# Keys, queries and output gates of an mLSTM: from wide products to seven block products of half the width

## The chip, the cores and the metric

One core of a Trainium2 chip runs the whole program. The metric is the device time of one execution in microseconds (us); the time before is the median of three runs. Engines: TensorE (PE, matmuls), VectorE (DVE), ScalarE (ACT), GpSimd (POOL), and SyncE (SP), which here only issues DMAs.

## The reference, cut to what matters

The program is two blocks of layers over 512 tokens of width 1024. The change concerns one layer of the second block, the mLSTM mixer:

```python
p = h @ w_in                       # 512 x 1024 times 1024 x 3088
q, k, v, o, ig, fg = jnp.split(p, [hk, 2*hk, 2*hk + D, 2*hk + 2*D, 2*hk + 2*D + 8], axis=-1)   # hk = 512, D = 1024
ig = 15 * tanh((ig + b) / 15);  logf = log_sigmoid(15 * tanh((fg + b) / 15))      # 8 heads
...
decay = exp(bcum_i - bcum_j + ii_j - m)          # causal, per head
scores = (q @ k.T) * decay
hh = rmsnorm((scores @ v + ...) / max(|den|, exp(-m)))
out = (sigmoid(o) * hh * hnorm_g) @ w_out
```

The values v (1024 columns), the keys and queries (512 each), the output gates o (1024) and the sixteen gate columns are all products of the same 512 x 1024 input h.

## The kernel before

All matmuls keep float32 accuracy by three passes: each operand is split (`split`, lines 189 to 192) into a rounded high part (ACT cast, L191) and the rest (DVE subtraction, L192), and `mm3` (lines 286 to 289) issues hi x hi (L287), hi x lo (L288) and lo x hi (L289). The transposed input lies in SBUF as `xt_hi` and `xt_lo`, 128 x 8 x 512, all eight pieces of the width times all tokens. Weights come by DMA in pieces of 512 KB into slots of a pool named `mid` (27 slots of 128 x 1024 floats, shared between lists "a" and "w"; `mid.share` moves slots between the lists).

A framework's scheduler lists the instructions of each engine once, before the run; on the chip each engine takes its list strictly in that order, waiting on semaphores. An instruction that waits therefore holds all behind it on its engine. The order around the change comes from the order of calls in `mlstm` and from the scheduler's own estimates.

In `mlstm` the calls run: `values()` (eight products, L1203 to L1206); `gates()`, whose `proj16` multiplies x by the 16 gate columns (16 matmuls, L242 to L245, then an add on DVE, L248) and whose chain runs on DVE and ACT (L1218 to L1241: tanh, log-sigmoid, a cumulative sum and a running maximum over 512 tokens by two scans, transposes); `keys(0)` and `out_gates(0)`; `attend(0)`; `keys(1)`, `out_gates(1)`; `attend(1)`. The scheduler lays some of the second half's products into attend(0).

`keys` and `out_gates` call `dense`: for each pair of 128-column tiles eight pieces of the width, three passes, each matmul 128 x 128 by 512 tokens. A call of either makes four such tiles: 4 x 8 x 3 = 96 matmuls of 512 columns; the four calls make 384.

Elsewhere (in the two `ffn` layers) the kernel has a second way to make products, `seven` (lines 380 to 445): it cuts x (by tokens and width) and the weight (by width and columns) into 2 x 2 blocks and forms seven block products instead of eight. A product is 2 x 4 x 3 = 24 matmuls of 256 columns, seven make 168. The weight's combinations are made on POOL (L411, L415, L420, L425, each a subtraction of two 128 x 1024 tiles in SBUF) and split like any weight; the results are summed out of PSUM on DVE (L421 to L441). The combinations of x are made once for all products by `Sums` (lines 352 to 375): two subtractions or additions on POOL (L363, L367), eight on DVE (L364 to L375, with four splits), the last of them written over `xt_hi` and `xt_lo` themselves.

The mlstm layer also carries a side job: `ada_sum(l, part)` accumulates a vector times a weight matrix on DVE (L573, 16 steps of 128 x 512, with a 256 KB DMA each), in steps that `ada_go` draws off at set places.

Of the kernel before, what the change touches and what calls it, by code (L numbers as in the profile page):

```python
# [13 lines left out]
AF = mybir.ActivationFunctionType  # L14
# [3 lines left out]
SEQ = 512  # L18
# [12 lines left out]
def kernel(ctx: ExitStack, tc: tile.TileContext, inp: dict, out: bass.AP):  # L31
# [88 lines left out]
    def blk(i):  # L120
        return slice(i * P, (i + 1) * P)
# [7 lines left out]
    def by_block(ap):  # L129
        return ap.rearrange("p (c t) -> p c t", t=P)  # L130
# [210 lines left out]
    def out_half(nk, o, ws):  # L341

        b = out_bank.next()
        for k in range(nk):
            mm3(b, *o(k), *ws(k), k == 0, k == nk - 1)
        return b
# [199 lines left out]
    def ada_open():  # L546
        ada_acc.extend(small.new("m", [512]) for _ in range(2))
        ada_in.append(Ring([small.new("m", [512]) for _ in range(2)]))
# [354 lines left out]
    def ple(l, then):  # L903
        small.share(c=11, f=6)
        mid.share(w=25, a=2)
        pT = [mid.new("a", [2, SEQ], F32R) for _ in range(2)]
        for tb in range(NB):
            t = small.new("f", [256])
            nc.sync.dma_start(t, inp["p"][l, 0, blk(tb), :])
            b = aux_bank.next()  # L910
            for c in range(2):
                T.transpose(b[:, blk(c)], t[:, blk(c)], ident)
            split(pT[0][:, :, blk(tb)], pT[1][:, :, blk(tb)], by_block(b[:, 0:256]))
            small.free(t)
        wp = [Weight(inp["ple_w"][l], 0, 2, [(hf * 512, 512)]) for hf in range(2)]
        ws = [Weight(inp["ple_gate_w"][l], 0, KD, [(hf * 512, 512)]) for hf in range(2)]
        for tb in range(NB):
            need(tb)
            sq = tiny(2)
            for hf in range(2):  # L920
                pw = out_half(2, lambda k: (pT[0][:, k, blk(tb)], pT[1][:, k, blk(tb)]), wp[hf])
                b = proj_tokens(ws[hf], tb, 512)
                sg = small.new("c", [512])

                S.activation(sg, b, AF.Tanh, scale=0.5)
                V.scalar_tensor_tensor(sg, sg, 1.0, pw, op0=add, op1=mult)
                xb = X[:, tb, half(hf)]
                V.scalar_tensor_tensor(xb, sg, 0.5, xb, op0=mult, op1=add)
                small.free(sg)
                then.half(tb, hf, sq)  # L930
            then.block(tb, sq)
        for w in (*wp, *ws):
            w.free()
        mid.free(*pT)
# [257 lines left out]
    def mlstm(then):  # L1192
# [5 lines left out]
        def values():  # L1198
            vs = [[small.new("f", [4, 129]) for _ in range(NB)] for _ in range(2)]
            for v in (*vs[0], *vs[1]):  # L1200
                G.memset(v[:, :, 128:129], 1.0)
            ws = [Weight(w_in, 0, KD, [(1024 + 512 * hg, 512)]) for hg in range(2)]
            for tb in range(NB):  # L1203
                need(tb)
                for hg in range(2):
                    S.copy(vs[hg][tb][:, :, 0:128], by_block(proj_tokens(ws[hg], tb, 512)))  # L1206
            for w in ws:
                w.free()
            return vs

        MX = mid.new("a", [2, SEQ], F32R)

        def gates():
            nc.sync.dma_start(b_if[0:16, :], inp["a_b_if_2"].rearrange("o n -> n o"))
            g16, t1, lf, bcum, cc, mx, one_row = rows = [small.new("c", [SEQ]) for _ in range(7)]
            fg = one_row
            a = proj16(w_in, 3072)
            V.tensor_scalar(g16[0:16, :], a[0:16, :], b_if[0:16, :], 1.0 / 15, op0=add, op1=mult)  # L1218
            S.activation(g16[0:16, :], g16[0:16, :], AF.Tanh)
            V.tensor_scalar(g16[0:16, :], g16[0:16, :], 15.0, None, op0=mult)  # L1220
# [22 lines left out]
            small.free(*rows)  # L1243

        def keys(hg):
            QT, KT = mid.new("a", [2, SEQ]), mid.new("a", [2, SEQ])
            for c0, dst, sc in ((256 * hg, QT, 1.0), (512 + 256 * hg, KT, 0.125)):
                bs = dense(w_in, 0, KD, [(c0, 256)], by_feat, (0, 1), 4)
                for c in range(2):
                    S.activation(dst[:, c, :], bs[c], AF.Copy, scale=sc)  # L1250
            return QT, KT

        def out_gates(hg):
            SG = Quad()
            for c in range(4):
                if c % 2 == 0:
                    bs = dense(w_in, 0, KD, [(2048 + 512 * hg + 128 * c, 256)], by_feat, (0, 1), 4)
                S.activation(SG[c], bs[c % 2], AF.Tanh, scale=0.5)
                V.tensor_scalar(SG[c], SG[c], 1.0, hn_half[:, 4 * hg + c : 4 * hg + c + 1], op0=add, op1=mult)
            return SG  # L1260

        def attend(hg, QT, KT, vv, SG, O):
# [49 lines left out]
            small.free(*vv)  # L1312
            SG.free()

        vv0, vv1 = values()
        mid.share(w=9, a=18)
        gates()
        ada_open()
        ada_sum(0, 4)
        qk0 = keys(0)  # L1320
        SG0 = out_gates(0)
        O = [Parts(), None]
        ada_cols(0, 4)
        ada_sum(0, 2)
        attend(0, *qk0, vv0, SG0, O[0])
        qk1 = keys(1)
        SG1 = out_gates(1)
        O[1] = Parts()
        attend(1, *qk1, vv1, SG1, O[1])
        mid.free(MX)  # L1330
        mid.share(w=19, a=8)
# [248 lines left out]
    rope_tables()  # L1580
    ple(0, NextX())
    dsa()
    ple(1, NextH(0, 0))
    mlstm(NextH(0, 2))
    ffn(0, NextH(1, 0))
    sgu(NextH(1, 2))
# [34 lines left out]
```

## Time and profile before

| | us |
|---|---|
| median of three runs (2270.41, 2270.75, 2275.05) | 2270.75 |
| the profiled execution | 2271.98 |
| its span in the trace | 2270.3 |
| mean granted clock of TensorE, share of full | 0.993 |
| PE busy | 2225.2 (98%) |
| DVE busy | 1466.6 (65%) |
| ACT busy | 974.1 (43%) |
| POOL busy | 237.1 (10%) |

The span is the time from the program's first to its last instruction in the trace; the run's own time is 1.7 us more. Busy shares are means over all layers, so what a change in one layer is worth must be read from that layer's stretch of the timeline: the mlstm's from the end of its values (1042.4) to the end of attend(1) (1203.2).

### The profile page before, as it was taken

The page shows a single profiled execution, that of the slowest core. Times are in us where ns is not written, and L with a number is a line of the kernel's source. Part 1 is how long each engine was busy: PE and PEld are TensorE (multiplying, and loading weights), DVE is VectorE, ACT ScalarE, POOL GpSimd, SP SyncE. Part 2 cuts the span into 40 slices and gives each one's busy share as a digit, 9 for nine tenths or more (in the row PEclk, how much of TensorE's full clock was granted, in tenths as well). Part 3 has the DMA queues.
Part 4 walks back from the last instruction along what each step waited for, and adds up shares of the span by engine and source line. Part 5 has one row for each costly group of instructions (what it writes and reads, how often), then busy time and mean ns, then how long its engine had stood idle before and what let it go on. Part 6 is the DMA issues. An engine that isn't in the chain of part 4 may idle for free.

```text
span 2270.3 us, 29339 instructions
## 1 busy us (share of the span) xinstructions
PE 2225.2 (98%) x11112; PEld 1825.5 (80%) x11112; DVE 1466.6 (65%) x2610; ACT 974.1 (43%) x1784; POOL 237.1 (10%) x209
## 2 busy tenths in 40 slices
PE   8999999999999999999999999999998999999998
PEld 6787788787777777887777888988787888898996
DVE  5655655844895857852637847767657748664765
ACT  4333344424344644343445534435524335443543
POOL 0000000100000000000211121312102201031130
PEclk9999999999999999999999999999999999999999
DMA  5343424322221124223413444352344534322322
GB/s 168 117 121 111 146 82 125 102 70 66 74 84 66 47 80 145 91 76 107 144 51 123 157 129 139 121 163 99 102 146 152 177 124 140 111 85 93 118 94 77
DMA packets 158063, 251.16 MB, mean 111 GB/s; under 512 B 13785, under 2 KB 59057, under 8 KB 157921
## 3 DMA queue, kind: packets, MB, share of 16 engines
q1 hardware_dynamic: 157920, 249.29, 34.7%
q8 instruction: 87, 1.43, 0.3%
q14 instruction: 56, 0.45, 0.1%
HBM read 247.15 MB, written 2.10 MB: 110 GB/s over the span
## 4 chain that ended last, share of the span: by engine, by line
PE 75%; DVE 11%; DMA 6%; ACT 3%; issue 3%; POOL 1%; SPq 0%; DVEq 0%; POOLq 0%; ACTq 0%
PE bank L287 22%; PE bank L288 22%; PE bank L289 22%; DMA small<-in_ada_w_dram 4%; DVE mid L192 4%; DVE small L573 2%; PE bank L1109 2%; PE bank L294 1%; ACT mid L191 1%; PE bank L1288 1%; POOL tiny_c L480 1%; PE bank L1293 1%; PE bank L1124 1%; DMA mid<-in_ffn_w_dram 1%; DMA mid<-in_b_w_in_dram 1%
## 5 line engine op out<-in xcount | busy, mean ns | idle before, releaser
L192 DVE TENSOR_TENSOR mid<-mid,mid 128x512 fp32r<-128x512 f32 (+2 forms) x530 | 514.2, 990 | 460.8 <-ACT mid L191 290.7
L191 ACT CAST mid<-mid 128x512 fp32r<-128x512 f32 (+2 forms) x530 | 420.0, 818 | 755.4 <-DMA mid<-in_ffn_w_dram 142.8
L287 PE MATMUL bank<-mid,mid 128*128 128x512 f32 (+1 forms) x1320 | 492.3, 373 | 6.5 <-DVE small L441 2.7
L288 PE MATMUL bank<-mid,mid 128*128 128x512 f32 (+1 forms) x1320 | 488.9, 370 | 1.5 <-DVE mid L192 1.5
L289 PE MATMUL bank<-mid,mid 128*128 128x512 f32 (+1 forms) x1320 | 488.1, 370 | 0.0
L287 PE MATMUL bank<-xt_hi,mid 128*128 128x512 f32 (+1 forms) x1216 | 428.6, 353 | 4.6 <-DVE small L1435 2.3
L289 PE MATMUL bank<-xt_hi,mid 128*128 128x512 f32 (+1 forms) x1216 | 426.1, 350 | 1.8 <-DVE mid L192 1.8
L288 PE MATMUL bank<-xt_lo,mid 128*128 128x512 f32 (+1 forms) x1216 | 425.6, 350 | 0.0
L287 PEld LDWEIGHTS bank<-mid,mid 128*128 128x128 f32 x1320 | 248.3, 188 | 55.7 <-DVE small L441 3.6
L288 PEld LDWEIGHTS bank<-mid,mid 128*128 128x128 f32 x1320 | 248.1, 188 | 45.6 <-DVE mid L192 2.1
L289 PEld LDWEIGHTS bank<-mid,mid 128*128 128x128 f32 x1320 | 248.1, 188 | 45.4
L287 PEld LDWEIGHTS bank<-xt_hi,mid 128*128 128x128 f32 x1216 | 230.1, 190 | 40.4 <-issue 5.1
L289 PEld LDWEIGHTS bank<-xt_hi,mid 128*128 128x128 f32 x1216 | 230.4, 190 | 34.4 <-DVE mid L192 2.4
L288 PEld LDWEIGHTS bank<-xt_lo,mid 128*128 128x128 f32 x1216 | 230.7, 190 | 32.2 <-issue 1.3
L287 PE MATMUL bank<-mid,xt_hi 128*128 128x512 f32 (+1 forms) x640 | 252.6, 395 | 0.0
L288 PE MATMUL bank<-mid,xt_hi 128*128 128x512 f32 (+1 forms) x640 | 250.4, 391 | 0.1
L289 PE MATMUL bank<-mid,xt_lo 128*128 128x512 f32 (+1 forms) x640 | 250.2, 391 | 0.0
L573 DVE SCALAR_TENSOR_TENSOR small<-small,c_act,small 128x512 f32<-128x512 f32 x168 | 134.1, 811 | 70.5 <-DMA small<-in_ada_w_dram 69.4
L289 PEld LDWEIGHTS bank<-mid,xt_lo 128*128 128x128 f32 x640 | 120.6, 188 | 26.7
L288 PEld LDWEIGHTS bank<-mid,xt_hi 128*128 128x128 f32 x640 | 120.7, 189 | 25.9 <-DVE mid L192 0.5
L287 PEld LDWEIGHTS bank<-mid,xt_hi 128*128 128x128 f32 x640 | 120.8, 189 | 25.3
L480 POOL TENSOR_TENSOR tiny_c<-tiny_c,minus_half 128x1 f32<-128x1 f32 (+1 forms) x68 | 54.5, 804 | 723.9 <-DVE tiny_c L494 377.2
(299 smaller groups left out, 2307.1 us busy)
## 6 DMA issues: line engine op xcount, KB each, us to landing
mid<-in_ffn_w_dram SPq DMA_DIRECT2D x128, 512.0 KB, 3.8
small<-in_ada_w_dram SPq DMA_DIRECT2D x192, 256.0 KB, 2.9
mid<-in_dsa_w_in_dram SPq DMA_DIRECT2D x36, 512.0 KB, 3.5
mid<-in_gla_w_in_dram SPq DMA_DIRECT2D x32, 512.0 KB, 4.3
mid<-in_b_w_in_dram SPq DMA_DIRECT2D x32, 512.0 KB, 3.7
mid<-in_a_w_in_dram SPq DMA_DIRECT2D x24, 512.0 KB, 3.8
mid<-in_gla_w_in_dram SPq DMA_DIRECT2D x32, 256.0 KB, 3.0
mid<-in_gla_w_out_dram SPq DMA_DIRECT2D x16, 512.0 KB, 3.7
```

The lines of the kernel that those rows point to most:

```text
L191: S.copy(hi, src)
L192: V.tensor_sub(lo, src, hi.bitcast(F32))
L287: T.matmul(o, lhsT=lh, rhs=rh, start=start, stop=False)
L288: T.matmul(o, lhsT=lh, rhs=rl, start=False, stop=False)
L289: turns.passed(o, T.matmul(o, lhsT=ll, rhs=rh, start=False, stop=stop))
L294: i = T.transpose(b[:, blk(c)], src, ident)
L480: G.tensor_tensor(r, v, minus_half[:, 0:m], op=ALU.pow)
L573: V.scalar_tensor_tensor(a, t, ck, a, op0=mult, op1=add)
L1109: T.matmul(b[:, :n], lhsT=QT[tb][:, blk(c)], rhs=KT[:, :n], start=True, stop=True)
L1124: T.transpose(b[:, blk(c)], es[c][:, blk(j)], ident)
L1288: T.matmul(sb[:, :n], lhsT=KT[pr, c // 2, blk(j)], rhs=QT[pr, c // 2, j * P :], start=True, stop=True)
L1293: T.matmul(nb[i // 2][:, (i % 2) * 129 : (i % 2) * 129 + 129], lhsT=Dm[j][:, blk(i - j)], rhs=vv[j][:, c, :], start=j == 0, stop=j == i)
```

## The change

`keys` and `out_gates` call `seven` in place of `dense`: four calls, 28 block products. `Sums()` is built behind the values and `proj16` and ahead of the chain of the gates (`gates(a16)`), and is freed behind the fourth call; both `attend` calls come after all of it. The side job's parts (0, 4) and (0, 2) are drawn off earlier, three steps at a time, in `ple(1)` and in `values`. The numbers of slots are other ones.

```diff
         def keys(hg):
-            QT, KT = mid.new("a", [2, SEQ]), mid.new("a", [2, SEQ])
-            for c0, dst, sc in ((256 * hg, QT, 1.0), (512 + 256 * hg, KT, 0.125)):
-                bs = dense(w_in, 0, KD, [(c0, 256)], by_feat, (0, 1), 4)
-                for c in range(2):
-                    S.activation(dst[:, c, :], bs[c], AF.Copy, scale=sc)
-            return QT, KT
+            QK = mid.new("a", [2, SEQ]), mid.new("a", [2, SEQ])
+
+            def done(t, n, b):
+                S.activation(QK[n][:, :, 256 * t : 256 * t + 256], b.rearrange("p (c t) -> p c t", c=2), AF.Copy, scale=(1.0, 0.125)[n])
+                small.free(b)
+
+            seven(w_in, 256 * hg, 512 + 256 * hg, sums, done)
+            return QK
 
         def out_gates(hg):
             SG = Quad()
-            for c in range(4):
-                if c % 2 == 0:
-                    bs = dense(w_in, 0, KD, [(2048 + 512 * hg + 128 * c, 256)], by_feat, (0, 1), 4)
-                S.activation(SG[c], bs[c % 2], AF.Tanh, scale=0.5)
-                V.tensor_scalar(SG[c], SG[c], 1.0, hn_half[:, 4 * hg + c : 4 * hg + c + 1], op0=add, op1=mult)
+
+            def done(t, n, b):
+                S.activation(SG.ts[n][:, :, 256 * t : 256 * t + 256], b.rearrange("p (c t) -> p c t", c=2), AF.Tanh, scale=0.5)
+                small.free(b)
+                if t != n:
+                    for c in (2 * n, 2 * n + 1):
+                        V.tensor_scalar(SG[c], SG[c], 1.0, hn_half[:, 4 * hg + c : 4 * hg + c + 1], op0=add, op1=mult)
+
+            seven(w_in, 2048 + 512 * hg, 2304 + 512 * hg, sums, done)
             return SG
...
+        ada_sum(0, 2, lambda: None)
+        ada_rate[0] = 3
         vv0, vv1 = values()
-        mid.share(w=9, a=18)
-        gates()
-        ada_open()
-        ada_sum(0, 4)
+        a16 = proj16(w_in, 3072)
+        ada_go()
+        ada_rate[0] = 0
+        mid.share(w=12, a=15)
+        sums = Sums()
         qk0 = keys(0)
+        gates(a16)
         SG0 = out_gates(0)
-        O = [Parts(), None]
-        ada_cols(0, 4)
-        ada_sum(0, 2)
-        attend(0, *qk0, vv0, SG0, O[0])
         qk1 = keys(1)
         SG1 = out_gates(1)
-        O[1] = Parts()
+        sums.free()
+        mid.share(w=10, a=17)
+        O = [Parts(), Parts()]
+        attend(0, *qk0, vv0, SG0, O[0])
         attend(1, *qk1, vv1, SG1, O[1])
```

What the layer now calls (unchanged, line numbers of before):

```python
# Sums.__init__ (lines 362 to 376); G is POOL, V is DVE, split is ACT then DVE
G.tensor_tensor(s2, lf[1][0], lf[1][1], op=add)        # L363
V.tensor_add(s1, hf[1][0], hf[1][1])                   # L364
V.tensor_add(s1, s1, s2)
split(*s[0], s1)
G.tensor_tensor(s3, lf[0][0], lf[1][0], op=sub)        # L367
V.tensor_sub(s2, s1, hf[0][0])                         # L368
V.tensor_sub(s2, s2, lf[0][0])
split(*s[1], s2)
V.tensor_sub(s1, hf[0][0], hf[1][0])                   # L371
V.tensor_add(s3, s3, s1)
split(*s[2], s3)
V.tensor_sub(s1, hf[0][1], s2)                         # L374
V.tensor_add(s1, s1, lf[0][1])
split(h[1][0], l[1][0], s1)

# seven, its first half
b11, b12, b22, b21 = load(0, c0), load(0, c1), load(1, c1), load(1, c0)
p = parts(b11)
G.tensor_tensor(b12, b12, b11, op=sub)                 # L411
...
S.copy(m1, product("11", p))
t2 = mid.new("w", [4, 256])
G.tensor_tensor(t2, b22, b12, op=sub)                  # L415
p = parts(b12)
...
p5 = product("s1", p)
p = parts(t2)
G.tensor_tensor(b11, t2, b11, op=sub)                  # L420
V.tensor_add(u, product("s2", p), m1)
...
```

How the lists of the engines changed. First DVE, from the gate columns' add backward (L248; its input comes from `proj16`). Before, three weight splits stand ahead of it:

```order
L192 TENSOR_TENSOR mid_561_8271<-mid_559_8269,mid_560_8270 128x1024
L192 TENSOR_TENSOR mid_564_8301<-mid_562_8299,mid_563_8300 128x1024
L192 TENSOR_TENSOR mid_567_8333<-mid_565_8331,mid_566_8332 128x1024
L248 TENSOR_TENSOR small_355_8202<-small_355_8202,bank0_61 16x512
L1218 TENSOR_SCALAR small_347_8175<-small_355_8202,b_if_157 16x512
```

In the change, the same place (mid_558, 560 and 562 are the low parts of the sums s1, s2, s3; mid_573 is the low part of b11, mid_576 that of b12 - b11):

```order
L364 TENSOR_TENSOR mid_563_8283<-xt_hi_70 128x1024
L365 TENSOR_TENSOR mid_563_8283<-mid_563_8283,mid_564_8284 128x1024
L368 TENSOR_TENSOR mid_564_8284<-mid_563_8283,xt_hi_70 128x1024
L192 TENSOR_TENSOR mid_558_8278<-mid_563_8283,mid_557_8277 128x1024
L369 TENSOR_TENSOR mid_564_8284<-mid_564_8284,xt_lo_71 128x1024
L371 TENSOR_TENSOR mid_563_8283<-xt_hi_70 128x1024
L192 TENSOR_TENSOR mid_573_8315<-mid_568_8306,mid_572_8314 128x1024
L192 TENSOR_TENSOR mid_560_8280<-mid_564_8284,mid_559_8279 128x1024
L372 TENSOR_TENSOR mid_565_8285<-mid_565_8285,mid_563_8283 128x1024
L192 TENSOR_TENSOR mid_576_8349<-mid_569_8308,mid_575_8348 128x1024
L248 TENSOR_TENSOR small_352_8274<-small_352_8274,bank0_61 16x512
```

Where three DVE operations on 128 x 1024 tiles stood ahead of the gates' add, there are ten in the change; the one that PE's first block product reads (mid_576) is the tenth.

PE behind `proj16` (its last two matmuls are L244 and L245). Before, the first product of the keys:

```order
L245 MATMUL bank0_61<-xt_hi_70,n16_72 48x512
L287 MATMUL bank1_62<-xt_hi_70,mid_560_8270 128x512
L288 MATMUL bank1_62<-xt_lo_71,mid_560_8270 128x512
L289 MATMUL bank1_62<-xt_hi_70,mid_561_8271 128x512
```

In the change (mid_557 and mid_558 are s1's two parts, mid_575 and mid_576 those of b12 - b11):

```order
L245 MATMUL bank0_61<-xt_hi_70,n16_72 48x512
L287 MATMUL bank1_62<-mid_557_8277,mid_575_8348 128x256
L288 MATMUL bank1_62<-mid_558_8278,mid_575_8348 128x256
L289 MATMUL bank1_62<-mid_557_8277,mid_576_8349 128x256
L287 MATMUL bank1_62<-mid_557_8277,mid_575_8348 128x256
...
L287 MATMUL bank0_61<-xt_hi_70,mid_572_8314 128x256
L288 MATMUL bank0_61<-xt_lo_71,mid_572_8314 128x256
L289 MATMUL bank0_61<-xt_hi_70,mid_573_8315 128x256
```

The product with s1 stands ahead of the one with x's own block (mid_572, mid_573), although `seven` is written the other way round; its third matmul reads mid_576.

ACT ahead of the first exponential of `attend(0)` (L1285 before, L1292 in the change). Before:

```order
L191 CAST mid_598_8836<-mid_597_8835 128x1024
L1258 ACTIVATE mid_572_8394<-bank1_62 128x512
L1285 ACTIVATE small_360_8573<-bank4_65,c_cols_158 128x512
```

In the change (mid_658, mid_661 and mid_664 are raw pieces of `w_out`, loaded into slots that the sevens give back; mid_665 is the cast of the third):

```order
L1260 ACTIVATE mid_629_9023<-small_372_9038 128x2x256
L191 CAST mid_659_9677<-mid_658_9676 128x1024
L1260 ACTIVATE mid_630_9024<-small_375_9187 128x2x256
L191 CAST mid_662_9695<-mid_661_9694 128x1024
L1260 ACTIVATE mid_629_9023<-small_373_9039 128x2x256
L191 CAST mid_665_9713<-mid_664_9712 128x1024
L1260 ACTIVATE mid_630_9024<-small_374_9125 128x2x256
L1292 ACTIVATE small_376_9264<-bank4_65,c_cols_158 128x512
```

Before, one cast of a weight of the same products stands there; in the change three casts of `w_out`'s pieces, the third of which waits for a DMA that can start only when a late product has given its slot back.

## Rows read from the trace of the kernel before

**Rows 1.** The profile's page, its parts 1 and 4 (busy time; share of the chain).

```profile
PE 2225.2 (98%) x11112; PEld 1825.5 (80%) x11112; DVE 1466.6 (65%) x2610; ACT 974.1 (43%) x1784; POOL 237.1 (10%) x209
...
PE 75%; DVE 11%; DMA 6%; ACT 3%; issue 3%; POOL 1%; SPq 0%; DVEq 0%; POOLq 0%; ACTq 0%
```

**Rows 2.** Windows: length, busy (x) of PE, PEld, DVE, ACT, POOL, clock, DMA share, GB/s.

```profile
1046.20:1094.50 48.30, 47.96 (x211) 37.14 (x209) 18.57 (x23) 18.89 (x25) 0.52 (x1) 1.00 0.36 105
1094.50:1133.40 38.90, 37.56 (x185) 25.76 (x184) 29.55 (x62) 17.75 (x64) 11.72 (x20) 1.00 0.52 160
1133.40:1167.20 33.80, 33.80 (x148) 27.14 (x146) 10.18 (x12) 11.13 (x15) 0.00 (x0) 1.00 0.22 74
1167.20:1203.20 36.00, 35.54 (x158) 24.01 (x158) 20.20 (x44) 18.47 (x64) 9.55 (x20) 0.91 0.13 44
1344.10:1384.30 40.20, 39.97 (x338) 39.71 (x336) 31.65 (x31) 25.12 (x35) 10.67 (x4) 1.00 0.32 105
2005.90:2045.90 40.00, 39.85 (x337) 39.60 (x336) 31.50 (x31) 25.06 (x35) 10.57 (x4) 1.00 0.33 105
```

**Rows 3.** Timeline of PE, end of the values, the gates' projection, first keys: start, us.

```profile
1035.44 0.40 PE L287 MATMUL bank<-mid,xt_hi 128*128 128x512 f32 x1
...
1042.40 0.40 PE L245 MATMUL bank<-xt_hi,n 128*48 128x512 f32 x1
...
1046.11 0.39 PE L287 MATMUL bank<-xt_hi,mid 128*128 128x512 f32 x1
```

**Rows 4.** Timeline of POOL in ffn(0): start, us, line, operation.

```profile
1280.98 2.42 POOL L367 TENSOR_TENSOR mid<-xt_lo 128x1024 f32<-128x1024 f32 x1 [12.96 <-PE bank L288]
...
1357.01 2.40 POOL L411 TENSOR_TENSOR mid<-mid,mid 128x1024 f32<-128x1024 f32 x1 [13.14 <-DMA mid<-in_ffn_w_dram]
1359.64 3.12 POOL L415 TENSOR_TENSOR mid<-mid,mid 128x1024 f32<-128x1024 f32 x1 [0.23 <-DMA mid<-in_ffn_w_dram]
1362.84 2.73 POOL L420 TENSOR_TENSOR mid<-mid,mid 128x1024 f32<-128x1024 f32 x1
```

**Rows 5.** Timeline of DVE beside those POOL products.

```profile
1279.91 1.23 DVE L365 TENSOR_TENSOR mid<-mid,mid 128x1024 f32<-128x1024 f32 x1
1281.05 3.44 DVE L192 TENSOR_TENSOR mid<-mid,mid 128x1024 fp32r<-128x1024 f32 x1
...
1358.47 2.01 DVE L192 TENSOR_TENSOR mid<-mid,mid 128x1024 fp32r<-128x1024 f32 x1 [2.08 <-ACT small L1390]
1360.41 0.68 DVE L431 TENSOR_TENSOR small<-small,bank 128x512 f32<-128x512 f32 x1
...
1363.83 2.82 DVE L192 TENSOR_TENSOR mid<-mid,mid 128x1024 fp32r<-128x1024 f32 x1
...
1367.17 1.21 DVE L192 TENSOR_TENSOR mid<-mid,mid 128x1024 fp32r<-128x1024 f32 x1
```

**Rows 6.** The page's part 6, DMA issues: count, KB each, median us to landing.

```profile
mid<-in_a_w_in_dram SPq DMA_DIRECT2D x24, 512.0 KB, 3.8
```

**Rows 7.** Timeline of ACT, casts of the keys' weights.

```profile
1043.53 1.05 ACT L191 CAST mid<-mid 128x1024 fp32r<-128x1024 f32 x1 [0.35 <-DMA mid<-in_a_w_in_dram]
```

**Rows 8.** Timeline of DVE through the chain of the gates.

```profile
1047.80 0.67 DVE L248 TENSOR_TENSOR small<-small,bank 16x512 f32<-16x512 f32 x1
...
1062.25 0.17 DVE L1241 COPY c_cols<-bank 128x32 f32<-128x32 f32 x1
```

**Rows 9.** Timeline of PE in ffn(0), a wait.

```profile
1433.89 0.55 PE L287 MATMUL bank<-xt_hi,mid 128*128 128x256 f32 x1 [2.33 <-DVE small L1435]
```

**Rows 10.** Windows of 2 us behind it: length, PE busy, granted clock.

```profile
1434.00:1436.00 2.00, 2.00 (x10) 0.50 0.00 0
1436.00:1438.00 2.00, 2.00 (x15) 0.73 0.00 0
```

**Rows 11.** Waits of PE, 1040 to 1210: in total, times, longest.

```profile
PE bank L1267 <- DVE small L1308: 1.3, 1, 1.3
PE bank L616 <- DVE small L1308: 0.5, 1, 0.5
```

More of the change, by code (lines that the diff above doesn't have):

```diff
@@ L920, in ple @@
             for hf in range(2):
+                ada_go(ada_rate[0])
                 pw = out_half(2, lambda k: (pT[0][:, k, blk(tb)], pT[1][:, k, blk(tb)]), wp[hf])
@@ L1205, in values @@
                 for hg in range(2):
+                    ada_go(ada_rate[0])
                     S.copy(vs[hg][tb][:, :, 0:128], by_block(proj_tokens(ws[hg], tb, 512)))
@@ L1211, in mlstm, with gates @@
         MX = mid.new("a", [2, SEQ], F32R)
-        def gates():
+        def gates(a):
             nc.sync.dma_start(b_if[0:16, :], inp["a_b_if_2"].rearrange("o n -> n o"))
@@ L1216, in gates @@
             fg = one_row
-            a = proj16(w_in, 3072)
             V.tensor_scalar(g16[0:16, :], a[0:16, :], b_if[0:16, :], 1.0 / 15, op0=add, op1=mult)
@@ L1582 @@
     dsa()
+    ada_open()
+    ada_col_steps(0, 4)
+    ada_rate[0] = 3
     ple(1, NextH(0, 0))
+    ada_go()
     mlstm(NextH(0, 2))
```

## The prediction, as put on record before the run

> **What bounds the kernel now.** I read the page first: PE is busy 98% of the span and holds 75% of the chain that ended last [rows 1]. Those are means, so the next view is windows over the layer that changes [rows 2]. From the gates' projection to the end of attend(1), PE is busy in 47.96 of 48.30 us, 37.56 of 38.90, 33.80 of 33.80 and 35.54 of 36.00, while DVE is busy in only 18.57 of the first 48.30 us and POOL in 0.52. So PE bounds this layer, and its matmuls leave the other engines room. The reader should see two things. Fewer matmul columns are worth their full time here, as long as PE stays fed. And before the change nothing in the layer asks POOL and DVE for much; the change does.
>
> The views after that are timelines: of PE at the place where the new work begins [rows 3], and of POOL and DVE in ffn(0), where the same `Sums` and `seven` already run [rows 4, 5]. The waits of PE [rows 11] say what is lost now: 1.3 and 0.5 us.
>
> **Gain on PE.** The window from 1133.40 holds 146 matmuls of 512 columns in its 33.80 us (its 148 records less two short transposes): 0.2315 us each [rows 2]. The 384 that go are 384 x 0.2315 = 88.9 us. Two whole sevens take 40.20 and 40.00 us in the two ffn windows [rows 2]; less two and one wide matmuls in them, that is 39.7 for 336 matmuls of 256 columns. Four calls are 672, or 79.5 us. Gain: **9.4 us**, and no more than that, since a block product saves one eighth of the columns and the rest goes to the shorter matmul's slightly longer time per column.
>
> **The first product waits.** PE takes its list in order. Behind the gates' projection (1042.40 to 1046.11 [rows 3]) it now finds the product with s1, whose third matmul, at 1046.35, reads the tenth DVE operation of the list. What can DVE have done by then? It cannot begin before about 1035.6, since the slots that the sums are written to are still read by the values' last products [rows 3]. One DVE operation on 128 x 1024 takes a step of 1.14 us (1279.91 to 1281.05 [rows 5]), so ten alone would take 11.4 and end near 1047.
>
> But POOL works beside it, and there the trace shows a lock. A POOL product takes 2.40 us when it is free [rows 4]. The DVE split issued at 1281.05, just behind POOL's start at 1280.98, lasted 3.44 us: it ended 1.09 us after POOL did [rows 4, 5]. The one issued at 1358.47 ended 1.07 us after POOL's product of 1357.01; the POOL product issued at 1359.64 then took 3.12, because that split ran first [rows 4, 5]. The split at 1363.83 took 2.82, again 1.08 beyond POOL's end at 1365.57; a free one takes 1.21 (at 1367.17), and the additions that read PSUM are not held (0.68 at 1360.41) [rows 5]. So two-input SBUF operations of DVE and POOL's products take turns, one and one, and their times add. In the list all ten DVE operations have two SBUF inputs, and five POOL products (L363, L367, L411, L415, L420) stand ready beside them: the weights land 3.8 us after their issue [rows 6], so about when L411's turn comes. 1035.6 + 10 x 1.14 + 5 x 2.40 = 1059.0, against 1046.35 for PE: **12.6 us** of wait. The bound below is no holding at all: L363 ends at 1038.0, nine more DVE operations end at 1048.3, and PE waits 2.0 us. I take the upper end, since the rows show the turns every time both engines had work. In a wait this long the clock falls: after 2.33 us of waiting in ffn(0) PE ran at half clock for some 3 us [rows 9, 10], 14 matmuls at about 0.21 in place of 0.118 us, or **1.4 us**. Between 0 and twice that.
>
> The Trainium skill (SBUF — State Buffer, "Who interferes with whom") states such an exclusive lock on a port pair, and adds that a DVE tensor_scalar in a 2-port mode takes it too; no run here shows one beside a POOL product, and what it would do is the third rival.
>
> **The gates' chain in the second half of the keys.** Its add (L248) now stands behind those ten operations, so the chain of eleven small operations (first at 1047.80, last at 1062.25, together 7.5 us [rows 8]) runs amid the splits of the first two sevens, as do the last four operations of `Sums` (4 x 1.14 = 4.6). Two sevens of ffn keep DVE 31.65 of 40.20 us, their holds included [rows 2]; 31.65 + 12.1 = 43.8, which is **3.6 us** more than PE needs. The chain's end is not awaited, but the weight splits behind it in DVE's list are. The bound below is nothing (some of the splits run ahead). Above: between the tenth operation and the second seven's last split DVE has 16 operations of 1.14, ten additions from PSUM of 0.65, the chain of 7.5 and, if each holds it, six or seven POOL products of 2.40; that is 47.8 against 37.1 of PE's work: 10.7 late.
>
> **The join to attend(0).** Three casts of `w_out` pieces now stand in ACT's list ahead of its first exponential. The third piece's DMA can start when the last product but one has given its slot back, 2.8 us (24 matmuls) before the sevens' end; it lands 3.8 us after that [rows 6] and is cast in 1.05 [rows 7]: **2.0 us** in which PE has nothing but attend's first matmuls. Below: nothing, if the slot comes free earlier. attend(0) also loses the 47 matmuls that the scheduler had laid into it; their time is counted in the gain, and what they covered may show: attend(1), without them, ran at a mean clock of 0.91 over 36.0 us [rows 2], a loss of up to 3.2 us, and attend(0) at 1.00. I count none of it, and 3.2 as the bound above.
>
> **The side job.** Its 32 steps of DVE work and loads move into `ple(1)` and the values, where DVE has idle time of tens of us and PE is the bound. Nothing, as long as DVE's splits there stay ahead; in the old place they cost nothing either. The slots' new numbers: nothing beyond what the join counts.
>
> **The sum**, against the profiled execution of 2271.98: -9.4 + 12.6 + 1.4 + 3.6 + 2.0 = +10.2, so 2282.2. The median of the runs shown is 1.2 below the profiled one, so the median after the change would be **2281.0**.
>
> **Rivals.**
> - *The turns don't bind, and the change is faster.* POOL's products come late (their slots or loads do), or DVE gets several operations in between, so that PE waits only 2.0 us at the first product and nothing after. Then -9.4 + 2.0 = -7.4: 2263.3. For it: in steady ffn windows PE is busy in 39.97 of 40.20 us with the same POOL products running [rows 2]. Against: there the operands are made ahead of need, here the chain starts from nothing at 1035.6. The point at which it decides is a total of waits of 9.4 us.
> - *The first wait is half.* If two of the five POOL products fall behind the tenth operation, the first wait is 12.6 - 4.8 = 7.8; with the clock's 1.4 and half of the next two terms that makes +2.6: 2273.4, no difference that can be told.
> - *More is held than I count.* The tensor_scalar operations of the gates' chain (L1218, L1220) wait for a POOL product too, up to 2 x 2.40 = 4.8 us, before a split that PE needs: 2286. Or attend(0) falls to half clock like attend(1): 3.2 more.
>
> **How the numbers follow.** A change of 0.2%, 4.5 us, is about what a measurement of this kernel can tell from none: below 2266.2 is faster, above 2275.3 slower. My case holds 0.55 (its own range 2274 to 2288, by the lower bounds of the second and third waits and the upper ones of the clock), the half wait 0.20, the free chain 0.17, more held 0.08. From these: faster 0.17, no difference 0.22, slower 0.61. The range must reach to the free chain at 2263 and to the extra holds near 2291.
>
> **What would show it.** In the changed profile: PE waits of about 12 us in one piece just behind the gates' projection, released by the DVE split L192; DVE operations of 3.4 to 3.6 us there, in turn with POOL products; the granted clock at half behind that wait; two sevens in about 39.7 us of PE work; a wait on DVE's splits in the second seven; one of about 2 us ahead of attend(0)'s scores. If the first wait is under 3 us, the lock does not govern this place and I am wrong in sign.

## The result and the profile after

The changed kernel takes 2285.92 us (median of six runs, 2281.36 to 2295.26) against 2270.58 for the kernel before on the same chips: a ratio of the means of 1.0082, 95% interval 1.0061 to 1.0104, so 14 to 24 us slower: 18.6 between the means, 15.3 between the medians. 2281.0 was forecast, slower by 10.2, in a range from 2263 to 2291. The profiled execution of the changed kernel took 2285.08, its span is 2283.3.

The page, parts 1 and 4, answers to [rows 1]:

```profile
PE 2217.9 (97%) x11400; PEld 1837.2 (80%) x11400; DVE 1538.2 (67%) x2662; ACT 992.0 (43%) x1804; POOL 288.9 (13%) x227
...
PE 70%; DVE 13%; DMA 7%; issue 5%; ACT 3%; POOL 2%; SPq 0%; DVEq 0%; POOLq 0%; ACTq 0%
```

PE is busy for 7.3 us less although the span is 13.0 longer: the work did shrink, and waits took its place. DVE's share of the last chain went from 11% to 13%, and POOL, now 2%, is on it. The layer itself, from the gates' projection to the first matmul behind attend(1) (L616), was 158.7 us before (1042.40 to 1201.10) and is 178.4 now. The difference, 19.7, is more than the 13.1 between the two profiled executions, since the trace of before has a slow stretch far ahead of the change (a mean clock of 0.95 from 558.6 to 667.6 us, 1.00 in the trace after, and the gates' projection 6.3 us later). Behind the layer the profiles differ as well: from L616 to the end, where every version runs the same calls, they took from 1065.7 us (e12, below) to 1077.0 (e4). So the layer's own length is the better measure in what follows, beside the time, and a few microseconds of it need not show in the time. Windows of the whole layer, before and after (columns as in [rows 2]):

```profile
1042.40:1201.10 158.70, 156.58 (x705) 114.89 (x704) 78.17 (x138) 68.49 (x168) 21.79 (x41) 0.98 0.34 104
```

```profile
1036.14:1214.56 178.42, 156.50 (x992) 129.93 (x990) 135.07 (x168) 86.74 (x189) 66.64 (x57) 0.91 0.22 70
```

PE is busy for the same 156.5 us in 178.4 (fewer columns, but more of them at the lower clock), DVE for 135 us in place of 78, POOL for 67 in place of 22, and the mean clock is 0.91, not 0.98. Where PE waited in the layer (what it waited for, us in total, times, longest):

```profile
PE bank L289 <- DVE mid L192: 7.4, 5, 4.5
PE bank L287 <- ACT mid L191: 6.5, 1, 6.5
PE bank L1240 <- DVE small L1233: 5.6, 1, 5.6
```

Before, [rows 11] had 1.8 us of waits that mattered; here these three sum to 19.5. The first two pieces stand just behind the gates' projection, as forecast, though one piece was expected there:

```profile
1046.46 0.58 PE L287 MATMUL bank<-mid,mid 128*128 128x256 f32 x1 [6.47 <-ACT mid L191]
...
1051.77 0.58 PE L289 MATMUL bank<-mid,mid 128*128 128x256 f32 x1 [4.52 <-DVE mid L192]
```

The second piece ends with the split that was named. The first ends with a cast on ACT, the high part of b12 - b11. POOL had made that difference by 1039.54 (L411, below), before PE needed it; but in ACT's list the cast stands behind the one of s2, which waited for DVE's L369, itself drawn out to 3.35 us:

```profile
1043.93 1.04 ACT L191 CAST mid<-mid 128x1024 fp32r<-128x1024 f32 x1 [5.89 <-DVE mid L369]
...
1045.36 1.05 ACT L191 CAST mid<-mid 128x1024 fp32r<-128x1024 f32 x1
```

And the turns of the two engines, DVE first, then POOL (start, us):

```profile
1029.38 3.30 DVE L364 TENSOR_TENSOR mid<-xt_hi 128x1024 f32<-128x1024 f32 x1 [13.89 <-PE bank L289]
1032.78 3.23 DVE L365 TENSOR_TENSOR mid<-mid,mid 128x1024 f32<-128x1024 f32 x1
1036.04 1.22 DVE L368 TENSOR_TENSOR mid<-mid,xt_hi 128x1024 f32<-128x1024 f32 x1
1037.19 3.44 DVE L192 TENSOR_TENSOR mid<-mid,mid 128x1024 fp32r<-128x1024 f32 x1
1040.55 3.35 DVE L369 TENSOR_TENSOR mid<-mid,xt_lo 128x1024 f32<-128x1024 f32 x1
1043.82 1.21 DVE L371 TENSOR_TENSOR mid<-xt_hi 128x1024 f32<-128x1024 f32 x1
1044.96 2.35 DVE L192 TENSOR_TENSOR mid<-mid,mid 128x1024 fp32r<-128x1024 f32 x2
1047.23 3.35 DVE L372 TENSOR_TENSOR mid<-mid,mid 128x1024 f32<-128x1024 f32 x1
1050.51 1.21 DVE L192 TENSOR_TENSOR mid<-mid,mid 128x1024 fp32r<-128x1024 f32 x1
```

```profile
1029.19 2.40 POOL L363 TENSOR_TENSOR mid<-xt_lo 128x1024 f32<-128x1024 f32 x1 [28.94 <-PE bank L288]
1031.55 3.38 POOL L367 TENSOR_TENSOR mid<-xt_lo 128x1024 f32<-128x1024 f32 x1
1036.32 3.22 POOL L411 TENSOR_TENSOR mid<-mid,mid 128x1024 f32<-128x1024 f32 x1 [1.40 <-PE bank L289]
1039.62 3.20 POOL L415 TENSOR_TENSOR mid<-mid,mid 128x1024 f32<-128x1024 f32 x1
1046.31 3.20 POOL L420 TENSOR_TENSOR mid<-mid,mid 128x1024 f32<-128x1024 f32 x1 [3.49 <-DVE mid L192]
```

Five of the ten DVE operations last 3.2 to 3.4 us, each beside one of the five POOL products; the two behind L371 (1044.96, x2) run at 2.35 for both, while POOL waits for its operand. The tenth ends at 1051.72.

### The profile page after: what moved, and what is told of

The parts are those of the page before. It is cut to its first block, busy times and chain, and to the rows that moved or that the text cites. A ratio compares the mean times of both kernels' runs of the same rounds, so it can differ in the third digit from the quotient of the medians.

```text
span 2283.3 us, 30056 instructions
## 1 busy us (share of the span) xinstructions
PE 2217.9 (97%) x11400; PEld 1837.2 (80%) x11400; DVE 1538.2 (67%) x2662; ACT 992.0 (43%) x1804; POOL 288.9 (13%) x227
## 4 chain that ended last, share of the span: by engine, by line
PE 70%; DVE 13%; DMA 7%; issue 5%; ACT 3%; POOL 2%; SPq 0%; DVEq 0%; POOLq 0%; ACTq 0%
PE bank L287 21%; PE bank L289 20%; PE bank L288 20%; DVE mid L192 4%; DMA small<-in_ada_w_dram 4%; DVE small L573 2%; PE bank L1110 2%; ACT mid L191 1%; PE bank L294 1%; PE bank L1300 1%; PE bank L1295 1%; POOL tiny_c L480 1%; DMA mid<-in_ffn_w_dram 1%; PE bank L1125 1%; POOL mid L411 1%
## 5 line engine op out<-in xcount | busy, mean ns | idle before, releaser
L192 DVE TENSOR_TENSOR mid<-mid,mid 128x512 fp32r<-128x512 f32 (+2 forms) x545 | 545.6, 1022 | 386.7 <-ACT mid L191 212.6
L191 ACT CAST mid<-mid 128x512 fp32r<-128x512 f32 (+2 forms) x545 | 435.4, 825 | 754.8 <-DMA mid<-in_ffn_w_dram 133.4
L287 PE MATMUL bank<-mid,mid 128*128 128x512 f32 (+1 forms) x1416 | 519.7, 367 | 11.0 <-ACT mid L191 6.5
L289 PE MATMUL bank<-mid,mid 128*128 128x512 f32 (+1 forms) x1416 | 516.6, 365 | 5.1 <-DVE mid L192 5.1
L288 PE MATMUL bank<-mid,mid 128*128 128x512 f32 (+1 forms) x1416 | 516.4, 365 | 1.5 <-DVE mid L192 1.5
L287 PE MATMUL bank<-xt_hi,mid 128*128 128x512 f32 (+1 forms) x1216 | 413.4, 341 | 5.9 <-DVE small L1445 3.3
L289 PE MATMUL bank<-xt_hi,mid 128*128 128x512 f32 (+1 forms) x1216 | 411.9, 339 | 5.3 <-DVE mid L192 5.3
L288 PE MATMUL bank<-xt_lo,mid 128*128 128x512 f32 (+1 forms) x1216 | 411.6, 339 | 0.0
L287 PEld LDWEIGHTS bank<-mid,mid 128*128 128x128 f32 x1416 | 267.0, 189 | 59.6 <-ACT mid L191 7.8
L289 PEld LDWEIGHTS bank<-mid,mid 128*128 128x128 f32 x1416 | 266.9, 188 | 50.8 <-DVE mid L192 5.6
L288 PEld LDWEIGHTS bank<-mid,mid 128*128 128x128 f32 x1416 | 266.8, 188 | 46.5 <-DVE mid L192 2.1
```

Of the source, the lines that this page charges most:

```text
L191: S.copy(hi, src)
L192: V.tensor_sub(lo, src, hi.bitcast(F32))
L287: T.matmul(o, lhsT=lh, rhs=rh, start=start, stop=False)
L288: T.matmul(o, lhsT=lh, rhs=rl, start=False, stop=False)
L289: turns.passed(o, T.matmul(o, lhsT=ll, rhs=rh, start=False, stop=stop))
```

## The experiments

A length of the layer, below, is always from the first matmul of the gates' projection to the first of L616 behind attend(1) (its line is 624 or 631 in some variants).

**Without POOL's products (e1).** `Sums` and `seven` get the engine as an argument, VectorE for the mlstm alone:

```diff
-        sums = Sums()
+        sums = Sums(V)
...
-            seven(w_in, 256 * hg, 512 + 256 * hg, sums, done)
+            seven(w_in, 256 * hg, 512 + 256 * hg, sums, done, V)
```

> The combinations of x and of the weights of the mlstm's four calls are made on VectorE, none on GpSimd; the two ffn layers keep theirs on GpSimd. Theory (the two engines take turns, 2.40 us for each GpSimd product): although VectorE gets five more operations of 1.14 us, the first wait of TensorE behind the gates' projection falls from 11.0 us (6.47 + 4.52) to about 6.5, behind a first block product that runs without one, and no VectorE operation there lasts over 1.3 us; time 4 to 8 us under the change, about 2280. Rival (VectorE's chain alone is too long, GpSimd holds nothing): the wait grows by five operations, to about 14 us, time 2288 or more.

Measured: 2270.28 (ratio to before 0.9998, 0.9983 to 1.0012): all of the loss gone, though DVE has 18 more operations. Layer 160.2. The same stretch of DVE and the waits of PE:

```profile
1031.66 1.22 DVE L364 TENSOR_TENSOR mid<-xt_hi 128x1024 f32<-128x1024 f32 x1
...
1039.73 2.35 DVE L192 TENSOR_TENSOR mid<-mid,mid 128x1024 fp32r<-128x1024 f32 x2
```

```profile
PE bank L287 <- ACT mid L191: 2.0, 2, 1.8
PE bank L289 <- DVE mid L192: 1.8, 1, 1.8
PE bank L287 <- DVE small L248: 1.4, 1, 1.4
...
PE bank L1240 <- DVE small L1233: 0.2, 1, 0.2
```

No operation lasts over 1.23. The first wait is 5.2 us in four pieces (theory: 6.5; rival: 14), and the wait for the gates' chain fell from 5.6 to 0.2. The gain in time was larger than forecast, 15 us, not 4 to 8: the turns had cost more than the first wait (5.8 us of it are gone, and 5.4 of the wait for the chain).

**POOL's products that nobody needs (e9).** e1 alone leaves a question: POOL's results also came later (2.40 us a product in place of 1.14), so the chain through them was longer. So e1 again, with POOL adding tiles of no consequence, two beside the sums and four in each call:

```diff
+        if left.junk is not None:
+            nc.gpsimd.tensor_tensor(left.junk, b22, b22, op=add)
```

> As the run without GpSimd's products, plus 18 products of the same size on GpSimd (two beside the sums, four in each call) that go to a tile that nothing reads. Theory (turns at SBUF: what GpSimd does holds VectorE, whoever needs the result): VectorE's two-input operations beside them last up to 3.4 us, the first wait grows from 5.2 us in four pieces to 9 us or more, time 2276 to 2290. Rival (the change was slow because GpSimd's results came late, 2.40 us in place of 1.14 each in the chain from the loads to the splits): nothing waits for these, so VectorE's operations stay at 1.2 us and the time at 2268 to 2273.

Measured: 2294.32 (1.0108, 1.0069 to 1.0146), 24 us over e1 and a little over the theory's range, layer 181.5. DVE, then POOL, in the first stretch:

```profile
1036.31 3.42 DVE L368 TENSOR_TENSOR mid<-mid,mid 128x1024 f32<-128x1024 f32 x1
...
1047.71 5.74 DVE L192 TENSOR_TENSOR mid<-mid,mid 128x1024 fp32r<-128x1024 f32 x2
```

```profile
1035.38 3.27 POOL L372 TENSOR_TENSOR mid<-xt_lo 128x1024 f32<-128x1024 f32 x1
...
1046.79 2.75 POOL L433 TENSOR_TENSOR mid<-mid 128x1024 f32<-128x1024 f32 x1
1049.62 2.75 POOL L440 TENSOR_TENSOR mid<-mid 128x1024 f32<-128x1024 f32 x1
```

The operations that last 1.22 in e1 last 3.42 when a POOL product stands beside them, though nothing reads its result; two splits together last 5.74 beside two products. PE's first wait is 12.6 us in one piece, for L248. In this stretch it is the turn that costs, not the late result: that much of the theory is shown. The whole 24 us was not taken apart; the tile that nothing reads also holds a slot that weights could have had.

**Only the sums' two products moved (e10)**, `sums = Sums(V)` alone.

> Only the two products of GpSimd in the sums of x go to VectorE, the weights' combinations stay on GpSimd. Theory: two of the five turns of the first wait are saved, at a price of two operations of 1.14 us: the wait falls by 2 to 4 us from 11.0, what follows stays as in the change; time 2280 to 2284. Rival (the sums' two are what holds all): as the run without GpSimd's products, 2268 to 2273.

Measured: 2286.52 (2279.35 to 2291.37; 1.0065, 1.0044 to 1.0087). The waits behind the projection fell to 5.2 us, more than expected, and the one for the gates' chain stayed at 5.3; layer 169.5. In time the run can't be told from the change; the theory's 2280 to 2284 was not reached, and behind the layer its profile is 3.4 us longer than the change's (1072.1 against 1068.7). So the sums' two products show in the waits and in the layer, and the weights' combinations, which stay on POOL here, still cost the 16 us by which the run is over e1.

**The gates' chain first (e3).** `gates(a16)` is called ahead of `Sums()`.

> The gates' chain is called ahead of the sums. Theory (the 5.6 us wait in the second call is for the chain, which stands behind the sums in VectorE's list): that wait falls under 1 us, the first wait stays 11 to 12, some splits get later by 1 to 3 us; time 2 to 5 us under the change. Rival (the sums and splits take VectorE's time in any order): a wait of 4 us or more stays in the second call, time as the change.

Measured: 2286.32 (1.0077, 1.0061 to 1.0093), the same time as the change. The wait for the chain fell to 2.3 us, the first stayed at 6.5 + 4.5, the layer is 172.9: 5.5 shorter, of which the time shows nothing. Between the theory's 1 and the rival's 4, so neither; a gain of that size is hidden by what lies outside the layer (behind it this profile is 6.8 us longer than the change's).

**The sums early (e2).** They are called inside `values`, behind the last block of x, and the part that is written over x is split in the first call, ahead of its last weight:

```diff
                 need(tb)
+                if tb == NB - 1:
+                    mid.share(w=20, a=7)
+                    made.append(Sums())
...
+        if left.fin:
+            left.fin()
         p = parts(b22)
```

> The sums of x are made as soon as the last block of x is there, beside the last values' products, and the one that is written over x is split last, inside the first call. Theory (the chain of the sums starts too late to be hidden): the first wait falls from 11.0 us to under 1.5, with it the half clock behind it (3 us), and the 5.6 us wait for the gates' chain to under 3; the layer from the gates' projection to the end of the second attention takes about 161 to 164 us where the change takes 178.9 and before 160.8; time 2267 to 2271. Rival (GpSimd's products beside the weights' splits are what holds TensorE, wherever the sums stand): the first wait stays over 5 us, time over 2278.

Measured: 2295.50 (1.0111, 1.0090 to 1.0132), no faster than the change (the two intervals overlap) where 2267 to 2271 was expected, so the theory of a late start falls as it was put. The layer is 173.5, 4.9 shorter than in the change; what the time has more lies ahead of it and behind it. POOL in the stretch, and PE's waits:

```profile
1046.57 2.41 POOL L417 TENSOR_TENSOR mid<-mid,mid 128x1024 f32<-128x1024 f32 x1 [24.77 <-DMA mid<-in_a_w_in_dram]
...
1051.55 3.24 POOL L426 TENSOR_TENSOR mid<-mid,mid 128x1024 f32<-128x1024 f32 x1
```

```profile
PE bank L1253 <- DVE small L1246: 5.8, 1, 5.8
PE bank L287 <- DVE small L248: 5.6, 1, 5.6
```

POOL's next product waits until 1046.57, 24.8 us, for a load, presumably since the sums' temporaries hold slots that the weights wanted (no run shows that apart). So three products fall beside and just behind the projection (1047.29 to 1051), where the splits of the weights stand, and the add L248 comes late again, 5.6 us for PE: DVE first waits 3.78 us for a cast of POOL's late result, and its two splits behind that last 5.79 by turns (2.35 in e1). ACT's copies of the values' banks now stand behind casts that wait for the sums, 2.2 us of PE in `values`.

**Early sums without POOL (e6)** is the same with VectorE as the engine.

> As the run without GpSimd's products, with the sums of x made beside the last values' products, the part written over x last. Theory (what is left of the first wait, 5.2 us in four pieces, is the sums' chain on VectorE): it falls under 1.5 us, time 2263 to 2267. Rival (the casts on ScalarE in the sums stand ahead of the copies that free the values' banks, and the weights land later for want of slots, as where the sums were made early with GpSimd): 3 us or more of waits stand ahead of or behind the gates' projection, time 2269 or more.

Measured: 2267.87 (0.9992, 0.9975 to 1.0009), layer 155.9. No wait is left behind the projection; what stays is for the gates' chain (L1253, the transposes) and at attention's scores (L1308):

```profile
PE bank L1253 <- DVE small L1246: 2.3, 1, 2.3
PE bank L1308 <- DVE small L1309: 2.2, 1, 2.2
```

Against e2, which differs in the engine alone, that is 27.6 us in the medians. The loads come as late in both (they are issued 7.0 us ahead of the projection), so it is not they that differ. With POOL's products gone the early start does what it was to do. The time lies a little over the theory's range and can't be told from e1 or before.

**The first keys by the wide products (e4, e8).** In e4, `keys(0)` is the old function again. Its wide products read x behind the writing of the last sum over it, so they must wait for it, and the first keys and queries are made from that sum's block in place of x's.

> The first keys and queries are made by the wide products, the other three calls by seven block products. Theory (the sums need some 20 us of cover, which 96 wide matmuls give): the first wait is under 1.5 us, the gates' chain is awaited under 2 us, the gain falls by a quarter (2.4 us); layer 161 to 166 us, time 2268 to 2273. Rival (the block products themselves lose, by GpSimd's products beside the splits, 3 us or more per call): the waits in the three calls come to 8 us or more, time over 2277.

Measured: 2290.40 (1.0094, 1.0078 to 1.0111). PE waits 11.5 us for the cast of that last sum, so the cover that was meant was not there, and the run tells nothing of the theory. In e8 the last part is written inside the second of the four calls, by the same `fin` as in e2, and the wide products have x whole.

> With GpSimd's products: the first keys and queries by the wide products, three calls by seven block products, and the last of the sums is written over x only inside the second call, so that the wide products need not wait for it. Theory (the sums want cover of some 20 us): the wait behind the gates' projection is under 1.5 us, time 2270 to 2276 (gain 7.1 of 9.4, the attentions' 5 us and some 2 us of waits in the calls stay). Rival (each call of block products loses 3 us or more to GpSimd's turns, cover or not): waits of 8 us or more in the three calls, time over 2278.

Measured: 2275.94 (1.0023, 1.0005 to 1.0041), layer 167.4; just inside the theory's range. The waits around the projection are 1.2 and 2.1 us (under 1.5 was expected), those of the three calls 4 more: cover takes most of the first wait, and what is left is not zero.

**The place of the first attention (e5, e7, e12).** In the change both attentions stand behind the four calls, and they take 66.9 us (1147.62 to 1214.56) where they took about 61.9 before (38.9 less 47 laid-in matmuls of 0.2315, and 33.9 to L616); 1.4 us of the difference are six matmuls of the output product that stand ahead of L616 now, 24 in place of 18. Called between the second and third call, without POOL's products (e5), with early sums too (e7), and in the change as it is (e12):

```diff
+        O = [Parts(), None]
+        attend(0, *qk0, vv0, SG0, O[0])
         qk1 = keys(1)
         SG1 = out_gates(1)
         sums.free()
         mid.share(w=10, a=17)
-        O = [Parts(), Parts()]
-        attend(0, *qk0, vv0, SG0, O[0])
+        O[1] = Parts()
         attend(1, *qk1, vv1, SG1, O[1])
```

> As the run without GpSimd's products, and the first attention is called between the second and the third call, as before the change. Theory (the two attentions, put end to end behind the last call, take 67 us to the last wait in place of about 62, for want of other matmuls between): they come back to 61 to 63, the half clock at their start goes, the layer falls from 160.2 to 154 to 157 us; time 2264 to 2267. Rival (the attentions cost 67 us wherever they stand): layer 159 to 161, time 2269 to 2272.

> The two edits together. If both theories hold their gains add: layer 150 to 153 us, time 2259 to 2263. If the early sums only move the wait, it is as the first attention between the calls alone, 2264 to 2267.

> The change with GpSimd's products as they are, and the first attention called between the second and the third call. Theory (the attentions' 5 us come from standing end to end, apart from GpSimd's turns): the waits of 11.0 and 5.6 us stay, the two attentions take 62 to 64 us in place of 66.9; time 2280 to 2284. Rival (attention between the calls falls to half clock, as in one of the two runs that had it without GpSimd's products): the attentions take 70 us or more, time 2288 or more.

Measured (the attentions less 24 laid-in matmuls of 0.1185): e5 2267.08 (0.9991, 0.9975 to 1.0007), layer 158.0, attentions 63.5. e7 2278.80 (1.0025, 1.0001 to 1.0050), layer 164.9, attentions about 75. e12 2293.50 (1.0135, 1.0071 to 1.0199), layer 184.1, attentions about 75. So e5 comes near its theory, but its time can't be told from e1's. e7 is 10.9 us slower than e6, which differs in the place alone, where a gain was expected. In e12 the rival holds (70 us or more, 2288 or more), though its time can't be told from the change's; its layer is 5.7 longer. The clock goes with the attentions' length, and the place alone does not decide it: the nine runs of e7, one and the same program, reach from 2268.68 to 2282.98 us, at mean clocks from 0.993 to 0.986. Windows of the first and second attention of e5, then of e7 (columns as in [rows 2]; the clock is the third from the right):

```profile
1092.14:1126.16 34.02, 32.76 (x161) 23.25 (x161) 22.19 (x48) 17.33 (x63) 10.06 (x20) 0.90 0.07 25
1163.22:1195.61 32.39, 31.92 (x156) 21.32 (x156) 21.13 (x47) 19.36 (x65) 9.89 (x20) 1.00 0.20 67
```

```profile
1091.70:1132.25 40.55, 37.65 (x162) 25.69 (x162) 22.34 (x48) 17.02 (x63) 9.97 (x20) 0.79 0.06 21
1169.36:1206.44 37.08, 36.62 (x156) 24.84 (x156) 21.37 (x47) 19.34 (x65) 9.92 (x20) 0.86 0.18 62
```

In e12 a part of the cause is to be seen, a POOL queue with the next call's products ahead of attention's masks (L1293); POOL, then DVE:

```profile
1107.11 3.22 POOL L420 TENSOR_TENSOR mid<-mid,mid 128x1024 f32<-128x1024 f32 x1
1112.28 2.34 POOL L425 TENSOR_TENSOR mid<-mid,mid 128x1024 f32<-128x1024 f32 x1 [1.95 <-issue]
1114.58 2.37 POOL L1293 TENSOR_SCALAR_AFFINE_SELECT small<-small 128x128 f32<-128x128 f32 x8
```

```profile
1108.04 2.97 DVE L1264 TENSOR_SCALAR mid<-mid,hn_half 128x512 f32<-128x512 f32 x2
...
1114.90 0.69 DVE L1296 TENSOR_TENSOR small<-small,bank 128x512 f32<-128x512 f32 x1 [2.16 <-POOL small L1293]
```

The masks begin at 1114.58 only, behind L420 and L425; DVE's L1296 waits 2.16 us for them, in a list where the pair L1264 ahead of it had been drawn out beside L420, and PE waits 6.9 us for L1296. In e7 there are no such products, and PE's waits in the first attention are 2.9 us in all against 1.3 in e5; why its clock stayed at half, from 1097.7 to 1113.7 us, was not settled.

**The gates' chain late (e11).** Early sums without POOL, and `gates(a16)` behind the third call.

> As the run without GpSimd's products and with early sums, and the gates' chain called behind the third call. Theory (the wait of 2.3 us for the chain in the second call, and the half clock behind it, are lost because its transposes stand in TensorE's list there): both go, the layer falls from 156.0 to 152 to 154 us; time 2263 to 2266, faster than before by some 5. Rival (the chain takes VectorE's time wherever it stands): a wait of 2 us or more in the third or fourth call or ahead of the attentions, time 2266 to 2270.

Measured: 2269.44 (twelve runs, 2261.20 to 2280.48; 1.0000, 0.9979 to 1.0021). The wait for the chain is 0.6 us, all waits of the layer are under 1.3 each, and the layer is 152.2 us in the profile, 6.5 under before. The profiled execution took 2263.85, inside the theory's range, but the median of the runs did not move. No version here can be told to be faster than the kernel before; the layer of this one is the shortest.

## Why the prediction was right, point by point

- **Gain on PE, 9.4.** As forecast. In the change, 72 matmuls of the third call take 8.53 us (1098.81 to 1107.34), 0.1185 each; 672 of them 79.6.
- **The first wait, 12.6.** Right in place, cause and size, though in two pieces, the first of them through ACT's list: 6.47 + 4.52 us, and the third matmul at 1051.77 is 11.7 late (it was due at 1040.08, one step of 0.23 and two of 0.12 behind the projection's last matmul at 1039.61). Five turns, ten operations, as counted; from POOL's start at 1029.19 to the tenth's end at 1051.72 they took 22.5 us, where 23.4 was forecast. e1 and e9 show the cause.
- **The clock behind it, 1.4.** Too small. 30 matmuls take 5.92 us from 1051.77 to 1057.69, 0.197 each: 2.4 lost. (The forecast's own 14 matmuls make 1.3, not 1.4.) The granted clock in that stretch, and behind the second wait:

```profile
1051.70:1057.70 6.00, 5.93 (x31) 5.93 (x32) 4.41 (x6) 1.68 (x2) 0.00 (x0) 0.57 0.10 37
1091.10:1095.10 4.00, 4.00 (x22) 3.93 (x21) 2.46 (x4) 2.85 (x3) 0.00 (x0) 0.59 0.24 83
1147.62:1214.56 66.94, 64.53 (x294) 42.88 (x293) 37.38 (x87) 35.14 (x126) 18.64 (x40) 0.92 0.16 53
```

- **The gates' chain, 3.6.** Mis-sized, and its path was another. The prediction said that the chain's end is not awaited, only the weight splits behind it. But its transposes (L1240) stand in PE's list in the middle of the second call, so PE waits for the chain itself: 5.63 us, 0.55 for a split, and some 1.6 at half clock behind it (21 matmuls from 1091.11 to 1095.17), 7.8 in all. The upper bound, 10.7, held. POOL had a part in the chain, too: L1230 lasted 2.23 us beside POOL's L425 (0.67 in e1), POOL's memset L1231 waited 0.60 for L1230, and the scan L1232 0.61 for the memset. Without POOL's products the wait is 0.2 (e1), with the chain called first 2.3 (e3).
- **The join, 2.0.** Too small, and mostly of another cause. The cast that was named does stand in the way: it runs at 1148.60, the exponentials from 1150.08, 2.5 us behind the last call's end, and PE then waits 1.43. But between them stands ACT's last activation of the gates, which needs a sum that DVE ends at 1149.23; without the cast the exponentials could have begun some 0.3 us earlier (an estimate from these rows), no more:

```profile
1148.55 0.68 DVE L441 TENSOR_TENSOR small<-small,bank 128x512 f32<-128x512 f32 x1
1149.55 0.63 ACT L1260 ACTIVATE mid<-small 128x512 f32<-128x512 f32 x1
```

  The two attentions take 66.9 us, so the term is 5.0, 1.4 of it work that only moved. The clock has the largest part in the rest: it was 0.68 and 0.57 in the first attention from 1151 to 1160 us, 0.84 and 0.82 in the second from 1190 to 1200. The half clock in attend(0), named as 3.2 and not counted, was there: 0.32 of 4 us and 0.43 of 5 make 3.4.
- **Left out:** waits for splits in the third and fourth call, 0.57, 1.25 and 0.53.
- Sum by what was measured: -9.4 + 11.7 + 2.4 + 7.8 + 5.0 + 2.4 = +19.9, the layer's 19.7. Against the runs' +15.3 (medians) or +18.6 (means) the forecast of +10.2 was low: every term but the first two came out over its estimate, toward its upper bound. The sign and the largest term follow from the mechanism that e1 and e9 show. That the median lies as near as 4.9 us to the forecast owes something to luck, since the chain and the join came out by other waits than those that were priced.
- **Rivals.** That the turns don't bind is refuted by the trace and by e9. The first wait was not half: all five products stood ahead of the tenth operation. That more is held than counted was partly so, though not at the tensor_scalar operations of the chain, beside which POOL had nothing to do (L1219 lasted 0.47 us at 1054.51). Those of the gates' activations (L1264) were held in the change, a pair for 1.92 us beside POOL's L425 (1111.21 to 1113.62); a pair alone takes 0.88:

```profile
1112.38 1.92 DVE L1264 TENSOR_SCALAR mid<-mid,hn_half 128x512 f32<-128x512 f32 x2 [0.70 <-ACT mid L1260]
...
1147.75 0.88 DVE L1264 TENSOR_SCALAR mid<-mid,hn_half 128x512 f32<-128x512 f32 x2
```

  The Trainium skill (SBUF — State Buffer, "Who interferes with whom") states that a tensor_scalar can enter a 2-port mode and that DVE in such a mode contends with GpSimd for the shared pair. The trace agrees in these rows.

## What to carry to other kernels

When two engines take turns, as these did, add their times over the stretch in which both have work, and not only their chains: ten operations of 1.14 us and five of 2.40 took 22.5 us here, and moving the slower engine's work to the faster one gave back all 15 us, although that engine then had more to do. A saving in matmul columns is worth its full time only while the operands are made ahead; where a new way of making them starts from nothing, give it cover first, and look at which instruction of each in-order list stands behind the new ones (here the gates' add, and the transposes that PE meets later). And what a wait costs is more than the wait: PE came out of these at half clock.

## What was not expected of the hardware

- A POOL addition whose two inputs are the same tile took 1.89 us where nothing held it (e9), 2.40 with two tiles:

```profile
1075.89 1.89 POOL L420 TENSOR_TENSOR mid<-mid 128x1024 f32<-128x1024 f32 x1 [23.52 <-DMA mid<-in_a_w_in_dram]
```

- Two DVE splits in a row (x2) are drawn out by two turns: 2.35 in e1 at 1039.73, 5.74 in e9. In these stretches DVE got two in a row only where POOL had nothing to do.
- The same attentions took 63.5 us at mean clocks of 0.90 and 1.00 (e5) or 75 at 0.79 and 0.86 (e7), with nearly the same lists. What decides between them no run shows.
